# Hybrid decoder step: the product A12 B21 moved from sixth to second place in each unit, and the order of work where the GLU, up and gate meet

## The chip, the core and the metric

One core of a Trainium2 chip runs one program. The metric is device microseconds of one execution; the lower the better. TensorE (PE) multiplies, VectorE (DVE), ScalarE (ACT) and GpSimd (POOL) work on vectors, SyncE (SP) issues most of the DMAs. Each engine works through its own list of instructions in the order in which the program wrote them, and waits where an operand of another engine is not yet there.

## The reference

One layer (DEPTH = 1) of a recurrent trunk, for a prompt of 512 tokens and 8 samples of one token, so 520 columns of activations in 2048 channels, all in float32:

```
xn  = rmsnorm(h);  y = S5 state space of xn;  z = gelu(y)
h   = h + z * sigmoid(z @ w_glu)                 # GLU, w_glu 2048 x 2048
xn  = rmsnorm(h)
u   = xn @ w_up;  gate = xn @ w_gate             # 2048 x 5632 each
c   = causal convolution of u over 3 tokens + b_conv
h   = h + (gelu(c) * gate) @ w_down              # 5632 x 2048
y   = rmsnorm(h)
```

The states of the other three mixers are copied through.

## The kernel before

**Split operands.** Every float32 operand is split into a high part (a copy that rounds to the format of the fast matmul, made by ACT) and a low part (the operand minus the high part, made by DVE). A product is three matmuls: high by high, high by low, low by high. The GLU and the first tiles of up and gate are plain (`products`): weight tiles of 8 x 128 rows and 256 columns, numbered 0 to 19 (0 to 15 GLU, 16 and 17 up, 18 and 19 gate), each split by `prepare(n)` before its 96 matmuls, its two parts in one of two buffer sets.

**Units.** The other 21 column blocks of up and of gate are done in 42 units, up and gate in turn. A unit multiplies a 256-column weight block by the activations with Strassen's scheme in Winograd's form: the weight is cut in four quarters A11, A12, A21, A22, the activations in B11, B12, B21, B22, and seven products of half size take the place of eight. S1 to S4 are sums of A quarters, T1 to T4 sums of B quarters. The activations' operands (B11, B22, B21, T1 to T4) are made once, ahead of the units: B11 and B22 in `fz`, three pairs and more in the `slots` that held the GLU's operand z, T4 in the place of the first half of the normalised rows. The weights' operands are made anew in each unit by `high(m)` and `low(m)`, where m counts through MAKING, seven per unit; some `low` also make the next sum (`early_sums`: S3 and S1). Four buffers (`ring`) go round: `unit` gives one back after each product and `high` takes it.

**Banks.** A unit uses three PSUM banks. USING is the order of the products, BANK says where each adds:

```
USING = ("A11", "S3", "S2", "A22", "S1", "A12", "S4")
BANK = {"A11": 0, "S3": 1, "S2": 0, "A22": 1, "S1": 0, "A12": 2, "S4": 0}
BEGINS = ("A11", "S3", "A12")
```

The products of BEGINS clear their bank, the others add to what stands there. After each product its bank is read (`assemble`, lines 1568 to 1582): A11, S3 and S2 are copied out by ACT, A22, S1 and A12 are added to an earlier block by DVE, S4 by ACT (up) or multiplied in by DVE (gate). Bank 0 is read after A11, after S2, after S1 and after S4, and goes on adding in between.

**Order in a unit.** After product k the program writes, in this order: the reading of its bank, `high(7n + k + 4)` on ACT, `low(7n + k + 3)` on DVE, and `between(k)`, which in gate units holds the convolution of the last two column blocks, and in the last unit (41) the split of the first tile of w_down and the first operands of the down projection.

**The seams.** While the GLU's last tile runs, its earlier blocks are already scaled by the norm's weights and split (`gained`). At up's step 4 PE sums the squares (`square_sums`, line 1406), then DVE makes the row scales as a diagonal and PE spreads them (`row_scales`). `first_steps` (row scaling, B11, B22, two differences) are called during up, `steps` (T3, T1, T2's high part, and the first weights) during gate, `last_steps` (B21, T4, the low part of T2) after it.

Of the kernel before, what the change touches and what calls it, by code (L numbers as in the profile page):

```python
# [1036 lines left out]

MAKING = ("A11", "A22", "S3", "S2", "A12", "S1", "S4")  # L1040
USING = ("A11", "S3", "S2", "A22", "S1", "A12", "S4")
OPERAND = {"A11": "B11", "S3": "T3", "S2": "T2", "A22": "T4", "S1": "T1", "A12": "B21", "S4": "B22"}
BANK = {"A11": 0, "S3": 1, "S2": 0, "A22": 1, "S1": 0, "A12": 2, "S4": 0}

# [3 lines left out]
def trunk_kernel(tc, x_prompt, x_sample, st_re, st_im, st_shift, st_wkv, st_gla, st_hgrn, st_conv, norm_mix, norm_ffn,  # L1048
# [8 lines left out]
    with ExitStack() as ctx:  # L1057
# [81 lines left out]
        def prepare(n):  # L1139
            if n not in parts and n < limit[0]:  # L1140
                split_steps = split(n)
                next(split_steps)
                split_steps.send("A")
                try:
                    split_steps.send("D")
                except StopIteration:
                    pass
# [12 lines left out]
        wa, wb = sets  # L1160
# [72 lines left out]
        def products(ps, n, block, after=None):  # L1233

            for k in range(2):
                prepare(2 * n + k)
                wh, wl = parts.pop(2 * n + k)
                for kk in range(8):
                    b, j = block(k, kk)
                    for i in range(2):  # L1240
                        mm6(ps[i], wh[:, b, i * 128:(i + 1) * 128], wl[:, b, i * 128:(i + 1) * 128],
                            xop(0, j), xop(1, j), k + kk == 0, k * 8 + kk == 15)
                    if after:
                        after(k * 8 + kk)
                prepare(2 * n + k + 2)

        def by_rows(k, kk):
            return kk, k * 8 + kk
# [71 lines left out]
        def low(m):  # L1320

            n, k = divmod(m, 7)
            if m < 0 or n >= len(units):
                return
            u, name = units[n], MAKING[k]
            w = made[n, name]
            V.tensor_tensor(w[:, 1], u.q[name], w[:, 0].bitcast(F32), op=OP.subtract)  # L1327
            if name == "A11":
                early_sums(n)
            elif name == "A22":  # L1330
                V.tensor_tensor(u.q["A22"], u.q["A22"], u.q["S3"], op=OP.subtract)
                u.q["S2"] = u.q["A22"]
            elif name == "A12":
                V.tensor_tensor(u.q["A12"], u.q["A12"], u.q["S2"], op=OP.subtract)  # L1334
                u.q["S4"] = u.q["A12"]
            elif name == "S4":
                fetch_unit(n + 2)
                if n == len(units) - 2:
                    limit[0] = len(jobs)
                    load_next()  # L1340
                    load_next()
# [21 lines left out]
        def gained(j):  # L1363
            b = rows[j // 8][:, :, j % 8]
            A.activation(two(xop(0, j)), b, AF.Copy)
            V.tensor_tensor(two(xop(1, j)), b, two(xop(0, j)).bitcast(F32), op=OP.subtract)

        for n in range(8):
            ps = [acc(), acc()]
            if n < 7:  # L1370
                load_x(n + 1)
            products(ps, n, by_rows, (lambda j: gained(j) if j < 14 else None) if n == 7 else None)
            if n == 0:
                small_operands()
            if n == 3:
                rows[1] = big([128, 2, 8, HALF], F32, "b2", "bq2")
            js = (n * 2, n * 2 + 1)
            sgs = [tmp("sg", i) for i in range(2)]
            for i in range(2):
                for b, sg in halves(ps[i], sgs[i]):  # L1380
                    A.activation(sg, b, AF.Sigmoid)
            for j, sg in zip(js, sgs):
                V.tensor_tensor(sg, sg, zcol(j), op=OP.mult)
                V.tensor_tensor(xs[j], xs[j], sg, op=OP.add)
                nc.sync.dma_start(h_res[j], xs[j])
            for i, j in enumerate(js):
                if j == 0:
                    A.activation(asq, xs[j], AF.Square)
                else:
                    sq = tmp("sq", i)  # L1390
                    A.activation(sq, xs[j], AF.Square)
                    (V if n == 7 else P).tensor_tensor(asq, asq, sq, op=OP.add)
            for j in js:
                A.activation(rows[j // 8][:, :, j % 8], two(xs[j]), AF.Copy, scale=gf[:, j:j + 1])
                xs.pop(j)
                if n == 7:
                    gained(j)

        row = {}

        def square_sums():

            pq = new_bank()
            for i in range(5):
                c0 = i * 128 if i < 4 else NT - 128
                PE.matmul(pq[:, i:i + 1], asq[:, c0:c0 + 128], ones[:, 0:1], start=True, stop=True)
            rsqrt(nc, rsm[:, 0], pq[:, 0:5], rsm[:, 1], D)
            dg = row["dg"] = hp.tile([128, 5, 128], F32, tag="u0", name="dg")
            V.tensor_tensor(dg, ident[:, None, :].to_broadcast([128, 5, 128]),
                            rsm[:, 0, :, None].to_broadcast([128, 5, 128]), op=OP.mult)  # L1410

        def row_scales():
# [3 lines left out]
            r = row["scale"] = hp.tile([128, NT], F32, tag="x4", name="rstd")  # L1416
            A.activation(r[:, 0:T], pq[0], AF.Copy)
            A.activation(r[:, T:NT], pq[1][:, 0:NB], AF.Copy)

        steps = []  # L1420

        def run(n=1):
            for _ in range(min(n, len(steps))):
                steps.pop(0)()

        fz = uzp.tile([128, 9216], R32, tag="uz", name="fz")
        ops = {}
# [8 lines left out]
        def high_of(name, r, h, place):  # L1436
            def step():
                ops[name] = place()
                A.activation(ops[name][0], rows[r][:, h], AF.Copy)
            return step  # L1440

        def low_of(name, r, h):
            def step():
                hi, lo = ops[name]
                V.tensor_tensor(lo, rows[r][:, h], hi.bitcast(F32), op=OP.subtract)  # L1445
            return step

        def summed(r, h, r2, h2, op):
            def step():
                V.tensor_tensor(rows[r][:, h], rows[r][:, h], rows[r2][:, h2], op=op)  # L1450
            return step
# [7 lines left out]
        def in_slots(i):  # L1459
            return lambda: [slot([128, 8, HALF], R32, "op", i + a) for a in range(2)]  # L1460

        def in_first_row():
# [3 lines left out]
        SUB, ADD = OP.subtract, OP.add  # L1466
        first_steps = [normed(0), high_of("B11", 0, 0, in_fz(0)), normed(1), high_of("B22", 1, 1, in_fz(2)),
                       low_of("B11", 0, 0), low_of("B22", 1, 1), summed(1, 1, 0, 1, SUB), summed(0, 1, 0, 0, SUB)]
        steps += [high_of("T3", 1, 1, in_slots(0)), low_of("T3", 1, 1), summed(1, 1, 0, 0, ADD),
                  high_of("T1", 0, 1, in_slots(2)), low_of("T1", 0, 1), high_of("T2", 1, 1, in_slots(4))]  # L1470
        last_steps = [high_of("B21", 1, 0, in_slots(6)), low_of("T2", 1, 1), low_of("B21", 1, 0),
                      summed(1, 0, 1, 1, SUB), high_of("T4", 1, 0, in_first_row), low_of("T4", 1, 0)]


        def conv(f, i, k):
# [21 lines left out]
        def in_up(j):  # L1497
            if j == 4:
                square_sums()
            elif j == 8:  # L1500
                row_scales()
                fetch_unit(0, (0,))
            if j > 8:
                first_steps.pop(0)()

        pu = [acc(), acc()]
# [11 lines left out]
        def in_gate(j):  # L1518
            if j == 0:
                for i in range(2):  # L1520
                    for b, u, r in halves(pu[i], u2[i][:, 128:128 + NT], rstd):
                        V.tensor_tensor(u, b, r, op=OP.mult)
            if j < 3:
                for i in range(2):
                    conv(i, i, j)
            elif j == 3:
                run(1)
                for i in range(2):
                    V.tensor_tensor(cv[i], cv[i], rstd, op=OP.mult)
            elif j == 5:  # L1530
                run(2)
            elif j == 7:
                run(2)
            elif j == 9:
                ring(wa, "wh")
                ring(wa, "wl")
                high(0)
                run(1)
                low(0)
            elif j == 11:  # L1540
                high(1)
            elif j == 13:
                low(1)

        pg = [acc(), acc()]
        products(pg, 9, by_pairs, in_gate)
        ring(wb, "wh")
        ring(wb, "wl")
        high(2)
        last_steps.pop(0)()  # L1550
        last_steps.pop(0)()
        low(2)
        high(3)
        for i in range(2):
            for b, t in halves(pg[i], cv[i]):
                V.tensor_tensor(t, t, b, op=OP.mult)
            nc.sync.dma_start(a_dram[i], cv[i])
        for st in last_steps:
            st()
        fetch_unit(1)  # L1560


# [29 lines left out]
        def gate_evict(name, bank):  # L1592
            if gates(name, bank) is not None:
                V.tensor_tensor(cv[0][:, h1], cv[0][:, h1], bank, op=OP.mult)
            elif name == "A12":
                V.tensor_tensor(cv[0][:, h0], cv[0][:, h0], g2[0][:, h0], op=OP.mult)


# [252 lines left out]
```

## Time and profile before

| | |
|---|---|
| median of 3 runs | 1942.37 us (1940.54 to 1943.3) |
| profiled execution | 1942.22 us |
| its span, first to last instruction | 1940.2 us |
| mean granted clock of PE | 0.969 |
| busy: PE, DVE, ACT, POOL | 92%, 63%, 41%, 9% of the span |
| chain that ended last: PE, DVE, DMA, ACT | 81%, 7%, 6%, 3% of the span |

The stages: the state space up to 293.6 us, the GLU to 485.4, the first tiles of up and gate to 536.5, the 42 units to 1406.6, the down projection and the final norm to the end. The profile's times are microseconds from the first instruction. In a timeline a row is a run of equal instructions: start, duration, engine, line, operation, output from inputs, shapes, count, and in brackets how long the engine stood idle before it and whom it waited for.

### The profile page before, as it was taken

To read this page: it belongs to the slowest core of one execution; us is meant where nothing else is said; L and a number is where in the kernel's file an instruction comes from. 1 tells how busy PE (TensorE), PEld (TensorE's weight loads), DVE (VectorE), ACT (ScalarE), POOL (GpSimd) and SP (SyncE) were. 2 spreads that over 40 slices of the span, in tenths; PEclk is the share of its full clock that TensorE was granted. 3 is DMA by queue.
4 is the path that set the end of the run, shared out by engine and by line. 5 is a ranking of instruction groups with operands and counts; after the bars stand their busy time and mean duration, and the time that the engine had idled before them with its cause. 6 is when DMAs were issued, how large, how long until landed. Compare 5 with 4: busy or idle time off the path is not lost.

```text
span 1940.2 us, 36289 instructions
## 1 busy us (share of the span) xinstructions
PE 1782.3 (92%) x15698; PEld 1757.3 (91%) x15698; DVE 1218.7 (63%) x1827; ACT 791.1 (41%) x1147; POOL 167.8 (9%) x172
## 2 busy tenths in 40 slices
PE   1874489999969999999999999999999999999996
PEld 1764478999969999999999999999999999999996
DVE  3999073324787887878878788787744333343344
ACT  3771273334445444454444544445512111221123
POOL 4688020111000000000000000000000000000000
PEclk9986799999979999999999999999999999999998
DMA  7435535443233544435444354443582433233313
GB/s 145 101 111 92 99 58 142 133 150 121 99 141 120 175 162 150 177 121 181 157 151 176 120 182 156 153 137 104 178 286 88 135 106 131 87 132 127 118 66 89
DMA packets 230044, 259.91 MB, mean 134 GB/s; under 512 B 33333, under 2 KB 207885, under 8 KB 228781
## 3 DMA queue, kind: packets, MB, share of 16 engines
q1 hardware_dynamic: 227490, 253.74, 41.6%
q10 hardware_dynamic: 2202, 3.83, 0.7%
q8 instruction: 123, 2.02, 0.4%
q14 instruction: 37, 0.30, 0.0%
q0 software_dynamic: 192, 0.03, 0.0%
HBM read 226.62 MB, written 60.49 MB: 148 GB/s over the span
## 4 chain that ended last, share of the span: by engine, by line
PE 81%; DVE 7%; DMA 6%; ACT 3%; issue 2%; SPq 0%; ACTq 0%; POOL 0%; DVEq 0%
PE bank L1353 43%; PE bank L1172 34%; PE bank L1777 2%; DMA kd<-kt 2%; DMA m<-kd 2%; DMA xs<-in_x_sample_dram 1%; ACT sbk L146 1%; DMA x<-in_x_prompt_dram 1%; DVE bp L663 1%; PE py L947 1%; DVE op L1445 0%; DVE b L1432 0%; PE bank L1671 0%; DVE m L142 0%; PE py L816 0%
## 5 line engine op out<-in xcount | busy, mean ns | idle before, releaser
L1353 PE MATMUL bank<-op,w 128*128 128x260 f32 x5040 | 618.1, 284 | 9.6 <-DVE w L1327 5.5
L1353 PEld LDWEIGHTS bank<-op,w 128*128 128x128 f32 x5040 | 612.5, 189 | 11.2 <-DVE w L1327 6.1
L1172 PE MATMUL bank<-act,wh 128*128 128x260 f32 x2496 | 400.0, 282 | 0.0
L1172 PEld LDWEIGHTS bank<-act,wh 128*128 128x128 f32 x2496 | 341.3, 188 | 0.0
L1318 ACT ACTIVATE w<-raw 128x1024 fp32r<-128x1024 f32 x252 | 266.1, 1056 | 168.2 <-PE bank L1353 86.6
L1327 DVE TENSOR_TENSOR w<-raw,w 128x1024 fp32r<-128x1024 f32 x252 | 305.7, 1220 | 24.4 <-ACT w L1318 23.3
L1131 ACT ACTIVATE wh<-raw 128x2048 fp32r<-128x2048 f32 x61 | 116.8, 1916 | 467.2 <-PE bank L1172 465.2
L1353 PE MATMUL bank<-fz,w 128*128 128x260 f32 x2016 | 250.8, 283 | 5.1 <-DVE w L1327 4.8
L1353 PEld LDWEIGHTS bank<-fz,w 128*128 128x128 f32 x2016 | 246.4, 189 | 5.7 <-DVE w L1327 5.0
L1172 PE MATMUL bank<-act,wl 128*128 128x260 f32 x1248 | 250.9, 282 | 0.0
L1135 DVE TENSOR_TENSOR wl<-raw,wh 128x2048 fp32r<-128x2048 f32 x60 | 137.5, 2292 | 165.7 <-ACT wh L1131 165.7
L1172 PE MATMUL bank<-z,wh 128*128 128x260 f32 x1280 | 209.1, 286 | 3.7 <-DVE cps L1268 2.7
L1172 PEld LDWEIGHTS bank<-act,wl 128*128 128x128 f32 x1248 | 192.1, 188 | 0.0
L1172 PEld LDWEIGHTS bank<-z,wh 128*128 128x128 f32 x1280 | 178.0, 191 | 4.7 <-issue 3.2
L1172 PE MATMUL bank<-z,wl 128*128 128x260 f32 x640 | 129.9, 285 | 0.0
L1753 DVE TENSOR_TENSOR h<-h,bank 128x260 f32<-128x260 f32 x80 | 29.6, 422 | 130.9 <-PE bank L1172 130.9
L1753 DVE TENSOR_TENSOR uh<-uh,bank 128x260 f32<-128x260 f32 x80 | 29.6, 422 | 115.1 <-PE bank L1172 115.1
L1172 PEld LDWEIGHTS bank<-z,wl 128*128 128x128 f32 x640 | 100.0, 191 | 0.0
L1318 ACT ACTIVATE w<-s 128x1024 fp32r<-128x1024 f32 x42 | 44.6, 1061 | 74.6 <-PE bank L1353 72.9
L816 PE MATMUL py<-m,uz 128*64 128x128 f32 x256 | 27.1, 394 | 45.5 <-DMA m<-kd 45.5
L816 PEld LDWEIGHTS py<-m,uz 128*64 128x64 f32 x256 | 23.9, 209 | 47.6 <-issue 47.4
L1334 DVE TENSOR_TENSOR raw<-raw 128x1024 f32<-128x1024 f32 x42 | 51.5, 1225 | 1.4
(352 smaller groups left out, 1838.8 us busy)
## 6 DMA issues: line engine op xcount, KB each, us to landing
raw<-in_ffn_w_down_dram SPq DMA_DIRECT2D x44, 1024.0 KB
raw<-in_ffn_w_up_dram SPq DMA_DIRECT2D x42, 1024.0 KB
raw<-in_ffn_w_gate_dram SPq DMA_DIRECT2D x42, 1024.0 KB
raw<-in_s_w_glu_dram SPq DMA_DIRECT2D x16, 1024.0 KB
a_dram<-cv SPq DMA_DIRECT2D x44, 260.0 KB
src<-a_dram SPq DMA_DIRECT2D x11, 1040.0 KB
x<-in_x_prompt_dram SPq DMA_DIRECT2D x16, 512.0 KB
m<-kd SPq DMA_DIRECT2D x8, 1024.0 KB
```

Of the source, the lines that this page charges most:

```text
L146: A.activation(dst, src, AF.Copy, scale=1.0 if scale is None else scale)
L663: V.tensor_tensor(t, b[:, :, None, :].to_broadcast([128, 4, 8, 16]), q.to_broadcast([128, 4, 8, 16]), op=OP.mult)
L816: PE.matmul(py[eh][g2 * 64:g2 * 64 + 64, e4 * 128:(e4 + 1) * 128], uo[o][:, eh * 4 + e4, g2, 0:64], m1s[o][:, (eh * 4 + e4) * 2 + g2], sta ...
L1131: A.activation(hi, raw, AF.Copy)
L1135: engine[e].tensor_tensor(lo, raw, hi.bitcast(F32), op=OP.subtract)
L1172: PE.matmul(ps[hf][:, 0:HALF], w, x[:, hf * HALF:(hf + 1) * HALF], start=first and i < 2, stop=last and i >= 4)
L1318: A.activation(w[:, 0], u.q[name], AF.Copy)
L1327: V.tensor_tensor(w[:, 1], u.q[name], w[:, 0].bitcast(F32), op=OP.subtract)
L1334: V.tensor_tensor(u.q["A12"], u.q["A12"], u.q["S2"], op=OP.subtract)
L1353: PE.matmul(bank, w[:, a, kk], x[:, kk], start=name in BEGINS and kk + i == 0, stop=kk == 7 and i == 2, skip_group_check=True)
L1753: V.tensor_tensor(t, t, x, op=OP.add)
L1777: PE.matmul(ps, w[:, kk, ni * 128:(ni + 1) * 128], x[:, kk, c0:c1], start=kk + i == 0, stop=kk == 3 and i == 2)
```

## The change

MAKING and USING get a new order: A12 is made and used second; the other six keep their order among themselves. The difference that turns A12 into S4 is now made after S2 rather than after A12. In the gate units the multiplication of the first half moves from A12's reading to S4's. OPERAND, BANK and BEGINS stay, and so does `unit`.

At the seam of GLU and up, tile 17 is split after the last GLU blocks and no longer before them. The row scales are spread at step 7 of up instead of 8, and the eight `first_steps` begin one step earlier. In gate the operands are made in a new order by a table `then`: B21, T3, the sum for T2, A11 and the difference for T4, T1, A12, T4; after gate A22, S3 and T2. They take other slots. `low(3)` is called after gate; `unit` calls it too in unit 0.

```diff
-MAKING = ("A11", "A22", "S3", "S2", "A12", "S1", "S4")
-USING = ("A11", "S3", "S2", "A22", "S1", "A12", "S4")
+MAKING = ("A11", "A12", "A22", "S3", "S2", "S1", "S4")
+USING = ("A11", "A12", "S3", "S2", "A22", "S1", "S4")
...
-                prepare(2 * n + k + 2)
+                if 2 * n + k != 15:
+                    prepare(2 * n + k + 2)
...
-            elif name == "A12":
+            elif name == "S2":
                 V.tensor_tensor(u.q["A12"], u.q["A12"], u.q["S2"], op=OP.subtract)
...
                     gained(j)
+        prepare(17)
...
-        steps += [high_of("T3", 1, 1, in_slots(0)), low_of("T3", 1, 1), summed(1, 1, 0, 0, ADD),
-                  high_of("T1", 0, 1, in_slots(2)), low_of("T1", 0, 1), high_of("T2", 1, 1, in_slots(4))]
-        last_steps = [high_of("B21", 1, 0, in_slots(6)), low_of("T2", 1, 1), low_of("B21", 1, 0),
-                      summed(1, 0, 1, 1, SUB), high_of("T4", 1, 0, in_first_row), low_of("T4", 1, 0)]
+        b21 = high_of("B21", 1, 0, in_slots(0)), low_of("B21", 1, 0)
+        t3 = high_of("T3", 1, 1, in_slots(2)), low_of("T3", 1, 1)
+        t1 = high_of("T1", 0, 1, in_slots(4)), low_of("T1", 0, 1)
+        t2 = high_of("T2", 1, 1, in_slots(6)), low_of("T2", 1, 1)
+        t4 = high_of("T4", 1, 0, in_first_row), low_of("T4", 1, 0)
+        then = {3: [b21[0]], 5: [b21[1]], 7: [t3[0], t3[1], summed(1, 1, 0, 0, ADD)],
+                9: [lambda: ring(wa, "wh"), lambda: ring(wa, "wl"), lambda: high(0), summed(1, 0, 1, 1, SUB),
+                    lambda: low(0)],
+                11: [t1[0], lambda: high(1)], 12: [t1[1]], 13: [t4[0], lambda: low(1)], 14: [t4[1]]}
...
+            elif j == 7:
+                row_scales()
             elif j == 8:
-                row_scales()
                 fetch_unit(0, (0,))
-            if j > 8:
+            if j > 7:
                 first_steps.pop(0)()
...
         high(2)
-        last_steps.pop(0)()
-        last_steps.pop(0)()
+        high(3)
+        t2[0]()
         low(2)
-        high(3)
+        low(3)
+        t2[1]()
         for i in range(2):
             for b, t in halves(pg[i], cv[i]):
                 V.tensor_tensor(t, t, b, op=OP.mult)
             nc.sync.dma_start(a_dram[i], cv[i])
-        for st in last_steps:
-            st()
...
             if gates(name, bank) is not None:
                 V.tensor_tensor(cv[0][:, h1], cv[0][:, h1], bank, op=OP.mult)
-            elif name == "A12":
                 V.tensor_tensor(cv[0][:, h0], cv[0][:, h0], g2[0][:, h0], op=OP.mult)
```

## Rows read from the trace of the kernel before

**Rows 1.** Windows of the unit stage: stretch, its length, busy PE, PEld, DVE, ACT, POOL, clock
```profile
620.00:700.00 80.00, 80.00 (x668) 79.90 (x666) 63.91 (x74) 40.19 (x62) 0.00 (x0) 1.00 0.45 159
...
1300.00:1390.00 90.00, 90.00 (x751) 89.91 (x750) 73.50 (x83) 44.36 (x68) 0.00 (x0) 1.00 0.39 126
```

**Rows 2.** Timeline of PE in units 1 and 2: start us, us, engine, line, operation
```profile
581.20 14.58 PE L1353 MATMUL bank<-op,w 128*128 128x260 f32 x120
595.62 5.91 PE L1353 MATMUL bank<-fz,w 128*128 128x260 f32 x48
```

**Rows 3.** Timeline of DVE in unit 1, a gate unit
```profile
590.10 0.42 DVE L1576 TENSOR_TENSOR g<-g,bank 128x260 f32<-128x260 f32 x1 [1.58 <-PE bank L1353]
...
592.92 0.42 DVE L1578 TENSOR_TENSOR g<-g,bank 128x260 f32<-128x260 f32 x1 [0.60 <-PE bank L1353]
...
596.79 0.42 DVE L1580 TENSOR_TENSOR g<-g,bank 128x260 f32<-128x260 f32 x1
```

**Rows 4.** Timeline of PE at the start of unit 0 (in brackets: idle before, releaser)
```profile
542.15 4.80 PE L1353 MATMUL bank<-fz,w 128*128 128x260 f32 x22 [4.81 <-DVE w L1327]
...
550.31 4.21 PE L1353 MATMUL bank<-op,w 128*128 128x260 f32 x22 [3.12 <-DVE w L1327]
558.55 0.80 PE L1353 MATMUL bank<-op,w 128*128 128x260 f32 x2 [4.03 <-ACT us L1570]
561.77 3.62 PE L1353 MATMUL bank<-op,w 128*128 128x260 f32 x15 [2.42 <-DVE w L1327]
```

**Rows 5.** Timeline of DVE from the GLU to unit 0
```profile
489.52 0.69 DVE L1383 TENSOR_TENSOR sg<-sg,uz 128x520 f32<-128x520 f32 x1
...
498.17 0.82 DVE L1409 TENSOR_TENSOR dg<-ident,rsm 128x640 f32<-128x640 f32 x1
502.78 2.29 DVE L1135 TENSOR_TENSOR wl<-raw,wh 128x2048 fp32r<-128x2048 f32 x1 [3.79 <-ACT wh L1131]
...
525.07 1.43 DVE L1522 TENSOR_TENSOR us<-bank,rstd 128x260 f32<-128x260 f32 x4
...
540.88 1.22 DVE L1327 TENSOR_TENSOR w<-raw,w 128x1024 fp32r<-128x1024 f32 x1
...
549.04 1.22 DVE L1327 TENSOR_TENSOR w<-s,w 128x1024 fp32r<-128x1024 f32 x1
...
558.25 2.32 DVE L1445 TENSOR_TENSOR op<-b,op 128x2080 fp32r<-128x2080 f32 x1 [2.06 <-ACT op L1439]
560.49 2.35 DVE L1327 TENSOR_TENSOR w<-raw,w 128x1024 fp32r<-128x1024 f32 x2
```

**Rows 6.** Timeline of DVE in unit 41, the last
```profile
1398.72 2.29 DVE L1135 TENSOR_TENSOR fz<-raw,fz 128x2048 fp32r<-128x2048 f32 x1 [2.32 <-ACT fz L1131]
...
1405.74 2.33 DVE L1611 TENSOR_TENSOR act<-src,act 128x2080 fp32r<-128x2080 f32 x1 [2.26 <-ACT act L1610]
1407.99 0.42 DVE L1580 TENSOR_TENSOR g<-g,bank 128x260 f32<-128x260 f32 x1
```

**Rows 7.** Timeline of PE from unit 41 into the down projection
```profile
1403.63 3.10 PE L1353 MATMUL bank<-fz,w 128*128 128x260 f32 x24
...
1408.12 7.04 PE L1172 MATMUL bank<-act,fz 128*128 128x260 f32 x57 [1.16 <-DVE act L1611]
```

**Rows 8.** Windows around three idle times of PE (the clock is third from the end)
```profile
494.00:500.00 6.00, 6.00 (x39) 6.00 (x39) 3.16 (x9) 3.05 (x5) 0.00 (x0) 0.72 0.29 106
564.00:566.00 2.00, 2.00 (x11) 2.00 (x10) 1.24 (x2) 0.00 (x0) 0.00 (x0) 0.50 1.11 370
1406.00:1408.00 2.00, 0.97 (x9) 0.76 (x7) 2.00 (x2) 2.00 (x2) 0.00 (x0) 1.00 1.05 395
```

**Rows 9.** Timeline of ACT where the GLU meets up
```profile
485.37 1.92 ACT L1131 ACTIVATE wh<-raw 128x2048 fp32r<-128x2048 f32 x1 [1.92 <-PE bank L1172]
```

**Rows 10.** Timeline of PE where up sums the squares
```profile
493.81 1.28 PE L1406 MATMUL bank<-ones,asq 128*128 128x1 f32 x10 [1.07 <-DVE asq L1392]
```

**Rows 11.** Timeline of ACT, the high part of T4
```profile
556.28 1.94 ACT L1439 ACTIVATE op<-b 128x2080 fp32r<-128x2080 f32 x1 [8.25 <-DVE b L1450]
```

More of the change, by code (lines that the diff above doesn't have):

```diff
@@ L1418, in row_scales @@
             A.activation(r[:, T:NT], pq[1][:, 0:NB], AF.Copy)
[L1420 to L1424, printed above, removed]
         fz = uzp.tile([128, 9216], R32, tag="uz", name="fz")
@@ L1526, in in_gate @@
             elif j == 3:
-                run(1)
                 for i in range(2):
                     V.tensor_tensor(cv[i], cv[i], rstd, op=OP.mult)
[L1530 to L1543, printed above, removed]
+            for step in then.get(j, ()):
+                step()
         pg = [acc(), acc()]
```

## Prediction

> **What bounds the kernel now.** I began with the windows of the long stage in which the 42 units run. TensorE (PE) is busy in all of the 80 us and all of the 90 us shown, at a granted clock of 1.00, the 2.4 GHz level; VectorE (DVE) is busy for 64 of the 80 us [rows 1]. The reader is to see that nothing can be won there, and that any wait put ahead of a matmul comes back whole in the total, because nothing later absorbs it. Then the timeline of PE in a unit: 120 matmuls go from 581.20 to 595.62 [rows 2], so one takes 0.1202 us and a product of 24 takes 2.88 us; seven make a unit of 20.2 us.
>
> Then the timeline of DVE in the same unit, unit 1. By its order of products S4 starts at 595.62 [rows 2], A12 one product earlier at 592.74, S1 at 589.85. The eviction of A22 starts at 590.10, that of S1 at 592.92 [rows 3]: a DVE eviction starts 0.18 to 0.25 us after the next product's first matmul. The eviction of A12 starts only at 596.79 [rows 3], 1.17 us after S4 began, for between the evictions of S1 and A12 DVE makes the low part of the next unit's A11 and the two early sums. That lateness is free now: A12 has bank 2 to itself.
>
> Last, the start of unit 0, where PE does stand still: 4.81, 3.12, 4.03 and 2.42 us, 14.38 us in all [rows 4]. Three of these waits are for low parts made by DVE; the third is of another kind. S2's first matmul adds into bank 0 and waited 4.03 us for ACT's copy of A11's block out of that bank [rows 4]. So an accumulation into a bank is held until the reader of what stood there is done. This row carries the prediction.
>
> **The change part by part.**
>
> *Order of use in the units.* A12 moves from sixth to second. Banks stay as they are, so the order of banks goes from 0 1 0 1 0 2 0 to 0 2 1 0 1 0 0. Until now A12 in bank 2 stood between S1 and S4, and S1's block had 2.88 us to be read. Now S4 follows S1 in the same bank, and its first matmul must wait for DVE to add S1's block. What is queued on DVE ahead of that: A22's eviction, waiting for the fifth product, then (same step of the unit) the low part of the next A11 and the early sums. This is the same run of three operations that today stands between the evictions of S1 and A12, 592.92 to 596.79 or 3.87 us from start to start [rows 3]. From the end of A22's product: 0.18 to 0.25 us to its eviction, 3.87 to the start of S1's, 0.42 for that [rows 3], and 0.05 until PE moves (a low part that ends at 549.04 + 1.22 = 550.26 releases a matmul at 550.31 [rows 4, 5]). That is 4.52 to 4.59 us, where S4 would be due after 2.88: a wait of 1.64 to 1.71. I take 1.68 us a unit. Behind it only PE is queued; DVE and ACT gain slack.
>
> Does the rest of the new order keep its due times? The tightest are the gate units. I walked DVE through one with 1.14 us from start to start for a low part (two of them in 2.35 [rows 5]) and, as estimates, 1.25 for a dependent sum and 0.67 for a convolution step: from the eviction of A12 (5.9 us into the unit) it has 7.9 us of work until A22's, due at 14.6, so 0.8 us to spare. S3's low part is done 5.1 us into the unit, needed at 6.0. S2's low part is done 7.5 in, needed at 8.9. No further wait comes out of it. For units 0 to 40: 41 x 1.68 = **+68.9 us**.
>
> *Unit 41.* There DVE's queue also holds a split for the down projection (2.29 us from 1398.72) and the low part of its first operand (2.33 us from 1405.74). The eviction that follows the latter starts at 1407.99 [rows 6] and is A12's; in the new order it is S1's. S4, which starts at 1403.63 now [rows 7], then cannot start before 1407.99 + 0.42 + 0.05 = 1408.46, +4.8. A12's eviction, now second, also holds DVE until 5.9 us into the unit, so the split comes up to 1.9 us later; my walk gives 6.0. The down projection then finds its operand ready, which gives back its wait of 1.16 [rows 7]. PE has stood 5.9 us, and after idle times like those at unit 0 the clock is 0.50, 1.2 GHz, for some microseconds [rows 8]; I charge 1.5. Sum 4.8 - 1.2 = 3.6 at least, 6.0 + 2.5 = 8.5 at most, taken as **+6.3 us**.
>
> *GLU to up.* Today tile 17's split stands ahead of the last GLU blocks on ACT (1.92 us from 485.37 [rows 9]), and DVE comes to the first block at 489.52 [rows 5]. Without it the sigmoids start at 485.37 and DVE at about 486.1, 3.4 us earlier. PE's 1.07 us wait for the sum of squares [rows 10] goes, and perhaps the fall of the clock after it, a mean of 0.72 over 6 us [rows 8]. But the split now stands behind the blocks and ahead of the row scales' arithmetic: ACT 492.2 to 494.1, DVE to 496.4. By the same spacing as now the scales' diagonal is done at 498.6, where it is done at 498.99 now [rows 5]. PE, early, waits for it. So tile 18's split, after which DVE is busy without a break, ends about 0.4 us earlier than 505.07 [rows 5]. Bounds: 0.4 gained; 0.7 lost if the clock falls all the same and the row scales come before tile 18's split.
>
> *Gate to unit 0.* From 525.07 [rows 5] to PE's last restart DVE is the chain. I counted its operations. Today: four low parts of weights, five of operands, two operand sums, three weight sums, four evictions, and a 2.06 us wait for T4's high part [rows 5], which ACT makes at 556.28 [rows 11]; PE restarts in the third product at 561.77 with 22 of its 24 matmuls to go [rows 4]. New: the same list with A12's low part for S2's, and one more, because the low part of S3 is made in the seam and again in unit 0, whose code is unchanged: +1.14. The wait for T4 shrinks to 0.85, since A12's low part stands in it: -1.21. The first product starts later: A11's low part, at 540.88 today [rows 5], comes behind both operand sums at about 543. The second, A12, hardly waits. The third, S3, needs the second making of its low part, again with 22 matmuls to go. So PE loses about 7.0, 0.6 and 6.7 us in place of 4.81, 3.12, 4.03 and 2.42: nothing gained beyond 0.1. With the GLU's 0.4, **-0.6 us**; at best all 14.38 us go, at worst +1.
>
> *Moves at no cost.* The gate's two multiplications both move to the unit's end, 0.42 us [rows 3], covered by PE's next product; uncovered it is 0.42 us in each of 21 gate units. Issues of DMAs keep their places in the units; unit 1's weights are asked for 1.5 us earlier, the second half of unit 0's 1.7 us later, both ahead of their first use.
>
> **Sum.** 68.9 + 6.3 - 0.6 = 74.6. The profiled execution took 1942.22 us (span 1940.2), the median of the runs is 1942.37: 1942.2 + 74.6 gives **2017 us**.
>
> **Rivals.**
>
> *The clock falls at the new waits.* 42 more idle times, each of about 1.5 us as the profile will show it (a matmul counts 0.28 us, its successor starts after 0.12). Against: the 1.16 us idle at 1406.97 left the clock at 1.00 [rows 7, 8]. For: 1.07 us, followed by ten matmuls with one column each [rows 10], was followed by 0.72 over 6 us, that is 2 x 0.28 x 6 = 3.4 us at half speed, 1.7 us lost [rows 8]. The new idle lies between. At every wait: 41 x 1.68 = 69 more, 2086 us; at every other, 2052 us. The Trainium skill, TensorE: Matmul & The Clock Gate, "A second HAM failure mode: psum-queue depth-cycling", says that many short idles between groups of matmuls, from going around the PSUM banks, can make the clock swing between its levels; by it the time would be the 2086 us above. The trace so far, with one dense case that kept its clock, bears it out only in part.
>
> *Not slower: S4 isn't held.* If the matmul into bank 0 went ahead without a wait for S1's eviction, the units would keep 20.2 us and the seams alone decide: 1942.2 - 0.6 = 1941.6 us. The place is the start of every S4, the price 1.68 us each, and it decides as soon as S1's block is still unread when S4 is due. Speaks for it: today no S4 waits in the units [rows 1]. Against: today A12 stands between, and the one matmul whose bank was still to be read waited 4.03 us [rows 4].
>
> *The seam pays.* If the second product really filled the holes of unit 0, up to 14.38 us would go and the time be 2003 us. Against: DVE's count above.
>
> **Chances.** 0.74 for the forecast (2011 to 2023: 41 x 1.64 to 41 x 1.71 is +-1.5, unit 41 +-2.5, seams -0.4 to +1.6), 0.09 for the clock falling at up to half of the waits (2025 to 2055), 0.08 for more than half, 0.07 for S4 not held, 0.02 for the seam. From 2002 (the seam's best) to 2055 lies 0.85. A difference under 0.2%, 3.9 us, can't be told from none. S4 not held: 0.05 within, 0.02 faster. Slower: 0.93.
>
> **What would show it.** The waits of PE should have a row for the matmul at L1353 released by DVE's addition at the eviction of S1, 41 times at about 1.5 us and once at some 6; two units that take 43.7 us in place of 40.4; at unit 0 idle times near 7.0, 0.6 and 6.7 us, the last restart near 561; the clock at 1.00 through the units. I am wrong if that row is missing, or if the windows of the units show a clock under 0.95.

## The result, and the profile after

The changed kernel takes 2022.05 us (median; 2020.36 to 2022.5), the kernel before 1942.32 on the same chip (1940.54 to 1943.3): a ratio of 1.041, 95% interval 1.0392 to 1.0428. The profiled execution of after took 2020.36 us, its span is 2018.5, 78.3 more than before's, and its mean granted clock 0.971 (before 0.969). Line numbers move with the edit: the matmul is L1354 (before L1353), the low part L1328 (L1327), the addition of S1's block L1566 (L1578).

PE's waits in after (waiting line, who released it, us in all, times, longest):

```profile
PE bank L1354 <- DVE g L1566: 37.3, 21, 5.8
PE bank L1354 <- DVE us L1566: 33.1, 21, 1.6
```

Neither row has a counterpart in the trace of before. They are S4's first matmul, held by DVE's addition of S1's block: 21 up and 21 gate units, 70.4 us in all, 5.8 of it in one wait. The chain that ended last, by engine, on the page of after:

```profile
PE 73%; DVE 15%; DMA 7%; ACT 3%; issue 2%; SPq 0%; DVEq 0%; ACTq 0%
```

PE's share was 81%, DVE's 7%: what PE lost, DVE has.

PE's timeline at the start of unit 0, in two middle units and in unit 41 (start, duration, line, shapes, count, idle before):

```profile
535.41 0.51 PE L1354 MATMUL bank<-fz,w 128*128 128x260 f32 x2 [0.36 <-ACT w L1319]
543.09 5.14 PE L1354 MATMUL bank<-fz,w 128*128 128x260 f32 x22 [7.17 <-DVE w L1328]
...
548.86 3.24 PE L1354 MATMUL bank<-op,w 128*128 128x260 f32 x24 [0.29 <-DVE w L1328]
560.29 5.90 PE L1354 MATMUL bank<-op,w 128*128 128x260 f32 x28 [8.20 <-DVE w L1328]
...
597.69 6.01 PE L1354 MATMUL bank<-fz,w 128*128 128x260 f32 x48 [1.58 <-DVE g L1566]
603.54 14.55 PE L1354 MATMUL bank<-op,w 128*128 128x260 f32 x120
619.67 6.01 PE L1354 MATMUL bank<-fz,w 128*128 128x260 f32 x48 [1.58 <-DVE us L1566]
...
1481.21 5.57 PE L1354 MATMUL bank<-fz,w 128*128 128x260 f32 x24 [5.76 <-DVE g L1566]
1486.57 3.70 PE L1172 MATMUL bank<-act,fz 128*128 128x260 f32 x28
```

In the middle units each row of 48 is S4 with the next A11, each row of 120 the five other products. From 603.54 the 120 need 14.42 us at the spacing of [rows 2], so S4 was due at 617.96; it starts at 619.67, 1.71 late. From S4 to S4 is 21.98 us, in before 20.20.

DVE's timeline at unit 0, in a middle unit and in unit 41:

```profile
554.31 1.22 DVE L1328 TENSOR_TENSOR w<-s,w 128x1024 fp32r<-128x1024 f32 x1
...
559.02 1.22 DVE L1328 TENSOR_TENSOR w<-s,w 128x1024 fp32r<-128x1024 f32 x1
...
615.33 0.42 DVE L1564 TENSOR_TENSOR us<-us,bank 128x260 f32<-128x260 f32 x1 [3.25 <-PE bank L1354]
615.67 1.22 DVE L1328 TENSOR_TENSOR w<-raw,w 128x1024 fp32r<-128x1024 f32 x1
616.80 1.22 DVE L1308 TENSOR_TENSOR s<-raw 128x1024 f32<-128x1024 f32 x1
618.06 1.22 DVE L1309 TENSOR_TENSOR raw<-raw 128x1024 f32<-128x1024 f32 x1
619.20 0.42 DVE L1566 TENSOR_TENSOR us<-us,bank 128x260 f32<-128x260 f32 x1
...
1478.49 2.32 DVE L1598 TENSOR_TENSOR act<-src,act 128x2080 fp32r<-128x2080 f32 x1 [2.25 <-ACT act L1597]
1480.73 0.42 DVE L1566 TENSOR_TENSOR g<-g,bank 128x260 f32<-128x260 f32 x1
```

The five middle rows are the queue that the prediction counted: A22's eviction, a low part, two early sums, S1's eviction. From start to start 3.87 us (615.33 to 619.20), as between the corresponding rows of before [rows 3]. The last ends at 619.62, S4 starts at 619.67.

Windows of after (stretch, length, busy PE, PEld, DVE, ACT, POOL, granted clock third from the end):

```profile
494.00:500.00 6.00, 6.00 (x46) 5.34 (x45) 3.02 (x8) 1.70 (x5) 0.40 (x3) 1.00 0.53 175
560.00:566.00 6.00, 5.71 (x28) 5.71 (x29) 3.98 (x5) 0.54 (x2) 0.00 (x0) 0.55 1.01 322
620.00:700.00 80.00, 75.27 (x624) 74.65 (x623) 59.46 (x69) 36.98 (x58) 0.00 (x0) 1.00 0.35 120
1300.00:1390.00 90.00, 82.54 (x679) 81.71 (x680) 66.18 (x77) 40.99 (x63) 0.00 (x0) 1.00 0.39 130
1481.00:1490.00 9.00, 8.79 (x52) 8.80 (x53) 5.58 (x6) 2.89 (x2) 0.00 (x0) 0.67 0.52 197
```

Where [rows 1] showed PE busy for 80.00 of 80 us it is now 75.27: three waits of 1.58 us, at an unchanged clock of 1.00. In the last window, behind the 5.76 us wait of unit 41, the clock is 0.67; it is 0.50 for S4's 24 matmuls (1481.2 to 1486.5 us).

ACT at the seam of GLU and up: the GLU's last sigmoid and then tile 17's split, which used to stand ahead of it [rows 9].

```profile
484.28 1.38 ACT L1382 ACTIVATE sg<-bank 128x260 f32<-128x260 f32 x4 [1.39 <-PE bank L1172]
...
491.04 1.90 ACT L1131 ACTIVATE wh<-raw 128x2048 fp32r<-128x2048 f32 x1
```

**Where the 78.3 us came from.** The time from the GLU's last block (484.28, in before 485.37) to S4 of unit 0 grew by 1.34 us (90.08 to 91.42); the 40 units from there to S4 of unit 40 by 40 x 1.787 = 71.5; from there to S4 of unit 41 by 5.86 (20.31 to 26.17); from that S4 to the down projection by 1.11 (4.25 to 5.36, not counting two matmuls that before had done ahead of its wait). That is 79.8. Of this, 1.09 us are missing in the span because the GLU's last block came earlier in this execution, by no effect of the change: the GLU's first matmul came 0.26 later (293.88, in before 293.62), and the GLU's code up to that block is the same. The clock from 310 to 330 us was 0.91, in before 0.83. A further 0.4 went after the units.

### The profile page after: what moved, and what is told of

Read it like the earlier page. It is cut to its first block, busy times and chain, and to the rows that moved or that the text cites. A ratio compares the mean times of both kernels' runs of the same rounds, so it can differ in the third digit from the quotient of the medians.

```text
span 2018.5 us, 36273 instructions
## 1 busy us (share of the span) xinstructions
PE 1789.7 (89%) x15698; PEld 1757.7 (87%) x15698; DVE 1213.9 (60%) x1828; ACT 791.9 (39%) x1147; POOL 167.7 (8%) x172
## 4 chain that ended last, share of the span: by engine, by line
PE 73%; DVE 15%; DMA 7%; ACT 3%; issue 2%; SPq 0%; DVEq 0%; ACTq 0%
PE bank L1354 36%; PE bank L1172 32%; DVE w L1328 3%; DMA kd<-kt 3%; DVE raw L1309 2%; DVE s L1308 2%; PE bank L1764 2%; DMA m<-kd 2%; DMA gt<-in_norm_mix_dram 1%; DMA x<-in_x_prompt_dram 1%; ACT sbk L146 1%; DVE bp L663 1%; PE py L947 1%; DVE op L1441 0%; DVE b L1428 0%
## 5 line engine op out<-in xcount | busy, mean ns | idle before, releaser
L1354 PE MATMUL bank<-op,w 128*128 128x260 f32 x5040 | 614.5, 283 | 8.5 <-DVE w L1328 8.5
L1354 PEld LDWEIGHTS bank<-op,w 128*128 128x128 f32 x5040 | 610.3, 189 | 8.9 <-DVE w L1328 8.9
L1354 PE MATMUL bank<-fz,w 128*128 128x260 f32 x2016 | 257.7, 287 | 77.9 <-DVE g L1566 37.3
L1354 PEld LDWEIGHTS bank<-fz,w 128*128 128x128 f32 x2016 | 248.2, 191 | 87.0 <-DVE g L1566 41.6
L1328 DVE TENSOR_TENSOR w<-raw,w 128x1024 fp32r<-128x1024 f32 x252 | 305.2, 1218 | 9.6 <-ACT w L1319 9.6
L1328 DVE TENSOR_TENSOR w<-s,w 128x1024 fp32r<-128x1024 f32 x43 | 52.5, 1221 | 22.4 <-ACT w L1319 22.4
```

The source lines that it names most:

```text
L1354: PE.matmul(bank, w[:, a, kk], x[:, kk], start=name in BEGINS and kk + i == 0, stop=kk == 7 and i == 2, skip_group_check=True)
```

## The experiments

The theory was that S4 waits for DVE's queue ahead of S1's eviction. The rivals: the time is lost in the seams, or in a clock that falls at the new waits. Each edit is against the changed kernel unless the text says otherwise.

**The old order in units 1 to 41, the new one in unit 0 and the seams.** MAKING and USING become a pair, one for unit 0 and one for the others, and the four operands go back to their old slots.

```diff
...
-            u, name = units[n], MAKING[k]
+            u, name = units[n], MAKING[min(n, 1)][k]
...
-            for k, name in enumerate(USING):
+            for k, name in enumerate(USING[min(n, 1)]):
...
```

> All seam changes kept, unit 0 in the new order, units 1 to 41 in the old order of products (operands in the old slots). Bank theory (S4 waits for the reading of S1's block out of bank 0, 1.79 us in each of 41 units and 6 in the last): the loss goes but for unit 0's own wait, 1942.3 - 0.4 + 1.8 = 1943.7 us, 1942 to 1946. Seam theory (the new order of the seam, its second making of S3's low part and its later loads cost the time): it stays near 2020 us.

Measured: 1944.94 us, ratio 1.0013 (1.0003 to 1.0023). PE's timeline:

```profile
564.34 13.81 PE L1354 MATMUL bank<-op,w 128*128 128x260 f32 x94 [8.20 <-DVE w L1328]
579.71 6.02 PE L1354 MATMUL bank<-fz,w 128*128 128x260 f32 x48 [1.56 <-DVE us L1566]
...
599.99 5.91 PE L1354 MATMUL bank<-fz,w 128*128 128x260 f32 x48
```

Unit 0, in the new order, still waits 1.56 us at S4; unit 1, in the old one, goes through. The total is 1.9 us above before's median of the same session (1943.00), which is unit 0's own wait. So the seams cost next to nothing, and the time is lost in the units.

**The early sums behind S1's eviction.** They leave the queue ahead of S1's eviction, where A22's eviction and one low part stay.

```diff
-            if name == "A11":
+            if name == "A11" and n == 0:
                 early_sums(n)
...
                 (up_evict, gate_evict)[n % 2](name, bank)
+                if name == "S1":
+                    early_sums(n + 1)
```

> As the changed kernel, but the two early sums of the next unit stand on DVE behind the reading of S1's block, not ahead of it. If the price is what DVE has queued ahead of that reading, S4 waits 0.24 + 0.42 + 0.05 us from the end of S1's product, with the restart 0.8 instead of 1.79: 2022 - 41 x 0.99 = 1981 us. If the price is that of two products in one bank as such, whatever DVE does, it stays at 2022 us.

Measured in two runs: 1979.95 us, ratio 1.0194 (1.017 to 1.0218). PE's timeline, then DVE's:

```profile
599.94 6.03 PE L1354 MATMUL bank<-fz,w 128*128 128x260 f32 x48 [0.52 <-DVE g L1568]
605.81 14.55 PE L1354 MATMUL bank<-op,w 128*128 128x260 f32 x120
620.88 6.01 PE L1354 MATMUL bank<-fz,w 128*128 128x260 f32 x48 [0.52 <-DVE us L1568]
```

```profile
617.60 0.42 DVE L1566 TENSOR_TENSOR us<-us,bank 128x260 f32<-128x260 f32 x1 [3.24 <-PE bank L1354]
617.94 1.22 DVE L1328 TENSOR_TENSOR w<-raw,w 128x1024 fp32r<-128x1024 f32 x1
620.40 0.43 DVE L1568 TENSOR_TENSOR us<-us,bank 128x260 f32<-128x260 f32 x1 [1.24 <-PE bank L1354]
620.74 1.22 DVE L1308 TENSOR_TENSOR s<-raw 128x1024 f32<-128x1024 f32 x1
```

DVE now stands idle for 1.24 us before S1's product ends, and starts the eviction as soon as PE lets it (620.40). Still S4 waits 0.52 us and the unit takes 20.93, 0.74 more than before. So the 1.79 us of the change has two parts: 0.74 for reading the bank at all (release, eviction, release, and 0.10 by which the matmuls behind a wait take longer), and 1.05 for what stands ahead of it in the queue.

**S1's block not read.** The addition of S1's block is left out, so the output lacks that term; the rest of the new order stays.

```diff
                 elif name == "S1":
-                    V.tensor_tensor(dst[1][:, h1], dst[1][:, h1], bank, op=OP.add)
+                    pass
```

> Leaves out the reading of S1's block (the addition of the sixth product's bank to the output half) in every unit; all else as the changed kernel. Bank theory: no S4 waits, units of 20.2 us; the last unit gives back about 5.7: 2022 - 73.4 - 5.7 = 1943 us, and no row of waits at S4. If the wait were for something else in the new order (a weight's low part, an operand), the time stays above 2000 us.

Measured: 1942.23 us, ratio 0.9994 (0.9984 to 1.0005). PE's timeline:

```profile
597.73 5.91 PE L1354 MATMUL bank<-fz,w 128*128 128x260 f32 x48
603.48 14.55 PE L1354 MATMUL bank<-op,w 128*128 128x260 f32 x120
617.87 5.92 PE L1354 MATMUL bank<-fz,w 128*128 128x260 f32 x48
```

No wait in front of S4, 20.14 us from S4 to S4. Everything else in the new order keeps its due times; the reader of S1's block alone carries the loss.

**Longer waits.** A11's low part is made twice for units 12 to 21, three times for units 22 to 31, four times for units 32 to 41, each time in the unit before, ahead of its S1's eviction. So S4 waits longer from unit 11 on.

```diff
-            V.tensor_tensor(w[:, 1], u.q[name], w[:, 0].bitcast(F32), op=OP.subtract)
+            for _ in range(1 + (max(n - 2, 0) // 10 if name == "A11" else 0)):
+                V.tensor_tensor(w[:, 1], u.q[name], w[:, 0].bitcast(F32), op=OP.subtract)
```

> As the changed kernel, but DVE makes the low part of the next unit's A11 once more ahead of the reading of S1 in ten units, twice more in the next ten, three times more in the next ten. If the clock holds, S4 waits about 1.6, 2.7, 3.9 and 5.0 us as the profile shows it, and the time is 2022 + 10 x 1.14 x (1 + 2 + 3) = 2090 us. Clock theory: from some length of the wait on the windows show 0.50 after it; each fall costs 1.7 to 2.5 us more, up to 2150 us if it falls in 20 to 30 of the units.

Measured in one run: 2145.15 us. PE's rows of S4 with the next A11, 48 matmuls each (line numbers one higher than in after):

```profile
798.49 6.01 PE L1355 MATMUL bank<-fz,w 128*128 128x260 f32 x48 [1.58 <-DVE us L1567]
...
821.75 7.41 PE L1355 MATMUL bank<-fz,w 128*128 128x260 f32 x48 [2.84 <-DVE g L1567]
...
846.39 6.01 PE L1355 MATMUL bank<-fz,w 128*128 128x260 f32 x48 [2.84 <-DVE us L1567]
...
869.65 7.36 PE L1355 MATMUL bank<-fz,w 128*128 128x260 f32 x48 [2.84 <-DVE g L1567]
...
1062.16 8.27 PE L1355 MATMUL bank<-fz,w 128*128 128x260 f32 x48 [4.10 <-DVE g L1567]
...
1197.54 8.80 PE L1355 MATMUL bank<-fz,w 128*128 128x260 f32 x48 [4.10 <-DVE us L1567]
...
1524.56 7.55 PE L1355 MATMUL bank<-fz,w 128*128 128x260 f32 x48 [5.36 <-DVE us L1567]
```

and windows of the same trace:

```profile
600.00:780.00 180.00, 166.80 (x1373) 165.15 (x1374) 130.29 (x152) 81.30 (x125) 0.00 (x0) 1.00 0.42 145
840.00:1040.00 200.00, 174.44 (x1393) 172.58 (x1392) 145.96 (x165) 82.99 (x126) 0.00 (x0) 0.97 0.40 139
...
1450.00:1550.00 100.00, 80.44 (x626) 79.61 (x624) 73.30 (x80) 39.37 (x61) 0.00 (x0) 0.89 0.31 99
```

Behind all eleven waits of 1.58 us the 48 matmuls take 6.01 us. Behind 2.84 they take 7.3 to 7.4 every second time, 6.01 otherwise, at a clock of 0.79 (869.6 to 876.9 us) and of 1.00 (846.3 to 852.3). The slow ones are all in gate units and the fast ones all in up units, so these rows do not tell whether the turn or the kind of unit decides. Behind 4.10 they take from 7.3 to 8.8, in up and gate units alike; behind 5.36 from 7.5 to 8.0. The longer waits cost 10 x (1.26 + 2.52 + 3.78) = 75.6 us as such, the slow rows 47 us more, summed over the 25 of them: 2022.05 + 75.6 + 47 = 2144.7, within 0.5 us of the measured time. So the rival of the falling clock is real, but not at the 41 waits of 1.58 us that this change makes; it acts at the one of 5.76 in unit 41.

**The change at the GLU alone**, in the kernel before: tile 17's split behind the last blocks, the row scales and `first_steps` one step earlier.

```diff
-                prepare(2 * n + k + 2)
+                if 2 * n + k != 15:
+                    prepare(2 * n + k + 2)
...
+        prepare(17)
...
```

> The kernel before with the changes of the GLU's end and of up's steps 7 and 8 alone. The prediction's term: PE's wait of 1.07 us for the sum of squares goes, DVE's unbroken work begins 0.4 us earlier, which is all that remains: 1942 us, no difference that can be measured. If instead PE's 1.07 us and the slow clock after it came back whole, 1939.5 us.

Measured: 1942.93 us, ratio 0.9997 (0.9988 to 1.0006). From the GLU's last block to PE's last restart in the third product it is 76.06 us, in before 76.40: 0.34 gained, which this measurement can't resolve. The wait of [rows 10] is gone and the clock from 494 to 500 us is 1.00, but both lay ahead of DVE's chain, which sets the end.

**S3's low part made once.** The changed kernel makes it after gate and again in unit 0; here the second making goes.

```diff
-                low(7 * n + k + 3)
+                if n + k:
+                    low(7 * n + k + 3)
```

> As the changed kernel, without the second making of S3's low part in unit 0. The prediction's count of DVE's operations: the third product starts 1.14 us earlier, 2021 us. If T2's low part or something else holds the third product, nothing moves.

Measured in one run: 2016.7 us. PE's timeline:

```profile
548.18 3.25 PE L1354 MATMUL bank<-op,w 128*128 128x260 f32 x24 [0.28 <-DVE w L1328]
554.90 4.47 PE L1354 MATMUL bank<-op,w 128*128 128x260 f32 x24 [3.48 <-DVE w L1328]
559.95 8.64 PE L1354 MATMUL bank<-op,w 128*128 128x260 f32 x70 [0.57 <-DVE w L1328]
```

The expectation was too small. The third product's last restart (554.90) is 71.28 us after the GLU's last block, in after (560.29) 76.01: 4.7 earlier, not 1.14. The second making lasts 1.22 us, but in after it stood at 559.02, behind T2's low part (2.24 to the next start) and four evictions (1.34); the first was done at 555.5. What it costs is its place in the queue. S2 then waits 0.57, and S4 of unit 0 comes 4.87 earlier.

**The banks apart.** If the wait comes from S1 and S4 in one bank back to back, an order with another bank between every pair should lose nothing. `USING` becomes A11 A12 S2 S3 S1 A22 S4, banks 0 2 0 1 0 1 0; S3's low part is made once, `low` comes ahead of `high`, and after gate A22's and S3's places change accordingly.

```diff
-MAKING = ("A11", "A12", "A22", "S3", "S2", "S1", "S4")
-USING = ("A11", "A12", "S3", "S2", "A22", "S1", "S4")
+MAKING = ("A11", "A12", "A22", "S2", "S3", "S1", "S4")
+USING = ("A11", "A12", "S2", "S3", "S1", "A22", "S4")
...
                 (up_evict, gate_evict)[n % 2](name, bank)
+                if n + k:
+                    low(7 * n + k + 3)
                 high(7 * n + k + 4)
-                low(7 * n + k + 3)
...
```

> As the changed kernel, A12 still second, but S2 third, S3 fourth, S1 fifth, A22 sixth: banks 0 2 0 1 0 1 0, so that no product adds into the bank of the one before it; S3's low part is made once. Bank theory: no waits at S4 (as with the order of before), units of 20.2 us. Unit 0's third product starts when S2's low part is there, about 557.7 where the changed kernel has 560.3 on its own clock; the last unit as before. 1942.3 - 0.4 - 2.6 = 1939 us, 1937 to 1943. Against it: S2's low part is due 0.4 us after it is made in every second unit; if it is late there, up to 20 x 0.5 = 10 us more.

Measured: 1940.28 us, ratio 0.9984 (0.9975 to 0.9994). PE's timeline:

```profile
556.85 0.58 PE L1354 MATMUL bank<-op,w 128*128 128x260 f32 x1 [4.12 <-ACT us L1559]
...
572.02 5.92 PE L1354 MATMUL bank<-fz,w 128*128 128x260 f32 x48
577.78 14.57 PE L1354 MATMUL bank<-op,w 128*128 128x260 f32 x120
592.20 5.92 PE L1354 MATMUL bank<-fz,w 128*128 128x260 f32 x48
```

A12 is second as in the change, S4 waits nowhere, and the unit takes 20.18 us. S4 of unit 0 comes 86.76 us after the GLU's last block, 3.3 earlier than in before. That the wait is gone speaks for the bank. The 3.3 us arise ahead of it, at the seam; which part of the seam's new order gives them is not separated.

**Two more seams on the banks apart.** Both keep the order and the banks of the run above. In the first, T1, T4 and the fetch of unit 1's weights move into unit 0, and T2's parts ahead; in the second, T4's two parts go behind gate, its low part behind S2's and S3's, and unit 1's weights are fetched ahead of gate's stores. Each diff shows a part of its edit, again against the changed kernel.

```diff
...
+        in_unit0 = {1: [t1[0], t1[1]], 2: [summed(1, 0, 1, 1, SUB), t4[0], t4[1], lambda: fetch_unit(1)]}
...
             def between(k):
+                for step in in_unit0.get(k, ()) if n == 0 else ():
+                    step()
...
```

> As banks_apart, and the operands made in the order of their use: T2 in gate, T1 after unit 0's second product, T4 after its third. If DVE's queue is what holds unit 0, its third product starts near 551.6, S1 follows without a wait, A22 waits some 3 us for T4: unit 0 ends about 7 us earlier than before, perhaps 1 to 5 of them given back while unit 1 waits for its weights, asked for 3 us later: 1935 us, 1934 to 1940. If not, it is at banks_apart's time.

Measured: 1939.66 us, ratio 0.9986 (0.9977 to 0.9994). S4 of unit 0 comes 82.75 us after the GLU's last block, 7.3 earlier than in before, but in unit 1 PE stands five times, 0.48 to 0.92 us each, and S4 of unit 1 comes 107.78 us after that block, in before 110.25. Two thirds of the gain are given back, as much as the expectation allowed.

```diff
...
         high(2)
-        high(3)
         t2[0]()
         low(2)
+        t4[0]()
+        high(3)
+        t2[1]()
         low(3)
-        t2[1]()
+        t4[1]()
+        fetch_unit(1)
...
-        fetch_unit(1)
```

> As banks_apart, but T4's low part stands behind S2's on DVE, and unit 1's weights are asked for ahead of the gate's stores. From banks_apart's trace: DVE loses 0.87 us of waiting and 2.24 of T4 ahead of the third product, which starts some 3 us earlier; the weights, which unit 1 waited for there (ACT 0.70 and 1.85 us), come some 2.5 us earlier too. If both hold, S4 of unit 0 starts 83.5 to 84 us after the GLU's end (before 90.1, banks_apart 86.8) and unit 1 gives nothing back: 1937 us, ratio about 0.997. If unit 1 waits for its weights again, it stays at banks_apart's time.

Measured: 1939.11 us, ratio 0.9982 (0.9972 to 0.9992). PE's timeline at the third and fourth products of unit 0:

```profile
558.94 3.12 PE L1354 MATMUL bank<-op,w 128*128 128x260 f32 x24 [0.75 <-DVE w L1328]
565.13 11.27 PE L1354 MATMUL bank<-op,w 128*128 128x260 f32 x70 [3.06 <-DVE w L1328]
```

Half right: S2, the third product, restarts for the last time 70.33 us after the GLU's last block (73.54 with the banks apart), but the fourth then stands for its own low part, 3.06 us, and S4 of unit 0 comes no earlier (87.63). The three versions take 2.5 to 3.7 us less than the kernel before, under 0.2%, and some 80 less than the changed one; their intervals overlap, so which is best stays open. From the GLU's last block to S4 of unit 1, each in its one profile, they are 3.3, 2.5 and 2.5 us ahead of before.

## Why the prediction was right

**The wait.** The place, the releaser and the queue came as predicted. With S1's block not read it is gone, with a shorter queue it is smaller, with a bank between it is gone: shown. Mis-sized was the price: 1.79 us a unit in place of 1.68, or 73.3 in place of 68.9 over the 41 units, above the 67.2 to 70.1 that its bounds of 1.64 and 1.71 give. Of the 0.11, 0.03 is the choice of the middle (S4 starts 1.71 late), and about the rest is a term that I lacked: the 48 matmuls behind a wait take 6.01 us, those without one 5.91 (unit 1 with the old order, 599.99). The time still fell in the range, near its upper end, because unit 41 and the seams used little of the room left for them: that is in part luck.

**Unit 41.** S4 came 5.86 us late (6.0 predicted). The down projection found its operand ready, as predicted. The clock cost more: S4's 24 matmuls took 5.57 us in place of 3.10 [rows 7], some 2.4 us lost where I charged 1.5. The wait that fell away gave back 1.3 (1.16 as the profile shows it), so the way from S4 to the down projection grew by 1.11. Together 7.0 in place of 6.3.

**The seams.** Idle times of 7.17, 0.29 and 8.20 us against 7.0, 0.6 and 6.7. The third is longer because PE was done with A12 sooner: 24 matmuls took 3.24 us at a clock of 1.00 (548.8 to 552.2 us), where the 22 of before's second product took 4.21 [rows 4] at 0.65. DVE, which sets the end, was as counted: from the GLU's last block to the third product's last restart 76.01 us in place of 76.40, 0.39 less where 0.6 was booked (my own terms, 0.4 and under 0.1, make 0.5). That the row for the clock after the GLU would rise from 0.72 to 1.00 was left open and came, at no gain. What I read wrongly there is the price of S3's second making. I booked 1.14 us; without it the third product's last restart comes 4.7 us earlier. The sum came out right because the whole list was counted, but without that second making the seam would have gained 5.3 us (0.4 and the 4.87 by which S4 of unit 0 came earlier).

**The clock in the units.** 1.00 in both windows shown, as forecast, and all 41 rows of 48 matmuls behind the waits take 6.01 us. The Trainium skill, TensorE: Matmul & The Clock Gate, "A second HAM failure mode: psum-queue depth-cycling", says that in one kernel short idles between groups of matmuls, from going around the banks, made the clock swing. The trace differs for the 41 waits of 1.58 us, which left it at 1.00, and agrees for those of 2.84 us, made on purpose, where it swings between 0.79 behind one wait and 1.00 behind the next.

**S4 not held** would have given 1941.6; the same order with the reader taken out gave 1942.23. The sum of that rival was good, its condition false.

**The sum.** 1.34 + 71.5 + 5.86 + 1.11 = 79.8 against the predicted 74.6, which is 5.2 too low: 4.4 the wait's size, 0.7 unit 41, 0.1 the seams.

## What to carry to other kernels

When the order of accumulations changes, write down the banks beside it: where two products in a row add into one bank with a read between them, the reader's whole queue stands in TensorE's path, and even an empty queue costs the release, the read and the release (0.74 us a unit here). A product in another bank between them hid all of it here. And what a doubled piece of work costs is read from its place in the queue, not from its duration: in unit 0, 1.22 us of work held a product back by 4.7.

## What the runs showed of the hardware

Not expected: a stream of 48 matmuls that begins behind a wait of 0.52 to 1.58 us takes 0.10 us longer than one that doesn't stop (6.01 to 5.91), at a granted clock of 1.00. Why is open. What an idle of PE between dense products cost in clock came in steps: none of the 1.58 us idles cost anything beyond that, every second one of 2.84 us (always in a gate unit) cost 1.3 to 1.4, every one of 4.10 us 1.3 to 2.8, and those of 5.36 us, longer, no more than 2.0. And the time at which the GLU ends varied from 483.6 to 488.7 us over the profiled executions with the same code ahead of it, which is of the size by which one kernel's runs differ (2020.36 to 2022.5, 1936.46 to 1945.4); a gain of 0.3 us at a seam can be read only from there on, not from the total.
